# Pairs of expert blocks, a summed norm, and seven raw weight buffers in an encoder layer with a product-key expert FFN

## The chip, the cores and the metric

The kernel runs on one core of one Trainium2 chip. The metric is the device time of one execution in microseconds, and the median over repeated executions is compared. Besides those, one execution was taken with the hardware profiler; all durations below come from it.

## The reference

One layer works on 512 tokens of 1,024 channels: a norm, one input projection, two token mixers (latent attention and a bidirectional state-space scan) merged by gates, an output projection, and then an expert FFN. The part in which most of the time lies is the FFN, which takes for each token and each of 8 heads the 16 best of 16,384 experts:

```python
def peer(h, w_query, sub_keys, w_down, w_up):
    q = (hf @ w_query).reshape(T, PEER_HEADS, 2, PEER_HALF)
    scores = jnp.einsum('thnd,hnkd->thnk', q, sub_keys)
    s_top, i_top = lax.top_k(scores, PEER_TOPK)
    cand = s_top[:, :, 0, :, None] + s_top[:, :, 1, None, :]
    cand_idx = i_top[:, :, 0, :, None] * N_KEYS + i_top[:, :, 1, None, :]
    best, pos = lax.top_k(cand.reshape(T, PEER_HEADS, -1), PEER_TOPK)
    idx = jnp.take_along_axis(cand_idx.reshape(T, PEER_HEADS, -1), pos, axis=-1)
    gate = jax.nn.softmax(best, axis=-1)
    # per token: act = gelu(x . w_down[idx]) * gate;  y = sum act * w_up[idx]

def reference(x, ...):
    h = rmsnorm(x, norm_mix)
    h_q, h_kv, k_r, u_ssm, gates = jnp.split(h @ w_in, IN_SPLITS, axis=-1)
    y_attn = mla(h_q, h_kv, k_r, ...) @ w_o_attn
    z = jax.nn.gelu(s5_bidir(u_ssm, ...)) @ w_glu
    y_ssm = (z[..., :SSM_WIDTH] * jax.nn.sigmoid(z[..., SSM_WIDTH:])) @ w_o_ssm
    g = jax.nn.sigmoid(gates)
    x = x + (g[:, :, 0, :] * y_attn + g[:, :, 1, :] * y_ssm) @ w_out
    x = x + peer(rmsnorm(x, norm_ffn), w_query, sub_keys, w_down, w_up)
    return rmsnorm(x, final_norm)
```

## The kernel before

**Arithmetic.** Every large product is made of fp16 halves: ScalarE writes the high half of a weight tile from its fp32 copy (`whi`), VectorE the low half (`wlo`), and TensorE multiplies three times (high by high, low by high, high by low). A weight tile of 128x1024 thus costs one load of 512 KB into a raw buffer, one ScalarE and one VectorE instruction, and the raw buffer is free again when VectorE has made the low half.

**The front** (`front`) computes the norm, the projections, both mixers and the merge. It begins with the sum of squares of x: 8 squares on ScalarE, each followed by 4 matmuls against a column of ones, then 4 square roots, a reciprocal, diagonal matrices and a matmul that spreads the result over the partitions; then the first two weight tiles, u0 and u1, meet the normed activations. `Stream` holds the list of all weight tiles of the front in the order of use and three raw buffers: `lo()` makes the low half of tile i and then issues loads up to tile i+3. Late in the front stand the attention's output projections (`oa0` to `oa7`, 256 KB each) and the GLU ones (`z0` to `z7`, with `os0` to `os7`), among which tiles of `w_out` (`wo`) and `w_query` (`wq`) that are kept for later are loaded and split.

**The experts** (`experts`, `Peer`) work in two ways. For the first 128 tokens the chosen rows of `w_down` and `w_up` are gathered with indirect DMAs on GpSimd (256 fetches of 128 rows, 512 KB each, into ten buffers) and used on VectorE, one instruction of 128x1024 for each fetch. The other 384 tokens are multiplied with all experts, in 128 blocks of 128. `ph1(i)` is the down product of block i (24 matmuls of 384 columns) and its gelu, which ScalarE writes into a slot: 13 slots of 128x384 in `area`, then 35 ring slots. `ph2(i)` is the up product (18 matmuls of 512 columns into six open PSUM banks); before it, `prep` loads the block's `w_up` and its gates (`Gb`, 192 KB, rows of 256 B from `gd` in HBM), VectorE multiplies slot and gates, ScalarE writes the high half `ph`, VectorE the low half `pl`. The gates in `gd` are made before by `onehot`: 24 tiles of 16 tokens, each four VectorE instructions of 128x2048 (`ej`, `eg` and twice `eg` by the gates) and four quarters of 8 small matmuls with a ScalarE copy each.

**What sets the order.** On TensorE, VectorE and ScalarE the order is written out: a list of units (ph1 and ph2) is run by `step()`, which prepares a unit up to three units ahead of its matmuls. While `onehot` is at work, the units are ph1 with the quarters shared out among them; 18 ph1 lie before that stage and `gtail` = 5 behind it, and all slots (35 + 13 = 48) are full when the stage of ph2 begins. So m = 48 - 18 - 5 = 25 ph1 lie within it. From there on ph2(i) follows ph2(i-1), with a ph1(nx) before it while nx < i + 35. A planner with a cost for each unit on TensorE (`tp`) and VectorE (`td`) puts the last top-k and then the gather's rows between the units, as long as `td < tp + lead`; `gcap` caps the rows per unit. DMA issues on SP and GpSimd are ordered by the framework, and SP's queue is in order: an issue that waits for a buffer holds up all behind it.

## Time and profile before

| | us |
|---|---|
| median of 3 runs | 1563.29 |
| lowest, highest | 1563.12, 1567.69 |
| the profiled execution | 1559.74 |
| its span, first to last instruction | 1558.0 |
| TensorE busy in the span | 1502.0 |
| VectorE busy in the span | 1296.7 |

The span is the time between the first and the last instruction; the execution's own time is 1.74 us longer, and the median of the timed runs lies 3.55 us above that. A busy TensorE is not always one at its peak, since matmuls are pipelined and their ends are modelled. In a table by stage the row gives, for each engine, busy time and instructions, then the granted clock of TensorE (1.00 is 2.4 GHz, 0.50 is 1.2 GHz), the mean busy share of the DMA engines and what they moved.

### The profile page before, as it was taken

The numbers are of one execution on the slowest core, as the hardware profiler recorded it, in microseconds if no ns is written. First come the engines' busy times: TensorE is split into PE (matmuls) and PEld (weight loads), VectorE is DVE, ScalarE is ACT, GpSimd is POOL, SyncE is SP. The second block draws the span as 40 slices with busy tenths as digits, with TensorE's granted clock in tenths as the row PEclk, the third lists the DMA queues.
The fourth block names the chain that finished last, engine by engine and source line by source line (L and its number), as shares of the span: only waits on it lengthen the run. The fifth ranks groups of instructions, "written<-read, shape, count | busy, mean of one in ns | idle before, by whom it ended". The sixth has DMA issues, their size and how long they took to land. (4 is left out here: it accounts for less than half of the span.)

```text
span 1558.0 us, 26141 instructions
## 1 busy us (share of the span) xinstructions
PE 1502.0 (96%) x9921; PEld 854.9 (55%) x9921; DVE 1296.7 (83%) x2571; ACT 742.9 (48%) x1117; POOL 374.5 (24%) x300
## 2 busy tenths in 40 slices
PE   8999999889989999999999999999999999999997
PEld 5547665448676567664444555555555555554433
DVE  4889688555999999986987988888888888888886
ACT  5456765554345479883432443333333333333334
POOL 0100100000000000000026654444555445444310
PEclk9999999999999999999999999999999999999999
DMA  5532622764103347769669999999999999999984
GB/s 192 129 97 49 94 69 90 238 201 157 42 15 125 125 140 284 277 252 332 177 218 389 385 385 366 349 347 348 367 344 354 348 345 368 351 311 323 324 270 147
DMA packets 201135, 378.64 MB, mean 243 GB/s; under 512 B 112305, under 2 KB 117809, under 8 KB 199985
## 3 DMA queue, kind: packets, MB, share of 16 engines
q1 hardware_dynamic: 159904, 231.50, 44.5%
q0 software_dynamic: 39520, 142.59, 26.9%
q10 hardware_dynamic: 1584, 2.88, 0.6%
q8 instruction: 77, 1.26, 0.3%
q14 instruction: 50, 0.40, 0.1%
HBM read 340.25 MB, written 36.14 MB: 242 GB/s over the span
## 5 line engine op out<-in xcount | busy, mean ns | idle before, releaser
L456 DVE SCALAR_TENSOR_TENSOR wlo<-raw,whi 128x1024 f16<-128x1024 f32 x256 | 311.9, 1220 | 125.3 <-ACT whi L453 124.2
L453 ACT ACTIVATE whi<-raw 128x1024 f16<-128x1024 f32 x256 | 262.0, 1050 | 168.7 <-DMA raw<-w_up 94.6
L1514 PE MATMUL ya<-whi,ph 128*128 128x512 f16 x768 | 291.9, 380 | 8.1 <-ACT ph L1502 6.1
L1515 PE MATMUL ya<-wlo,ph 128*128 128x512 f16 x768 | 291.8, 380 | 2.9 <-DVE wlo L456 2.6
L1516 PE MATMUL ya<-whi,pl 128*128 128x512 f16 x768 | 291.8, 380 | 1.0
L1545 POOL DMA_INDIRECT row<-w_dn,gidx x78 | 104.7, 1342 | 625.4 <-ACT whi L453 537.2
L543 PEld LDWEIGHTS <-wlo 128*128 128x128 f16 x1272 | 124.6, 98 | 111.7 <-DVE wlo L493 9.9
L541 PEld LDWEIGHTS <-whi 128*128 128x128 f16 x1272 | 124.6, 98 | 105.1 <-ACT whi L485 11.3
L542 PEld LDWEIGHTS <-whi 128*128 128x128 f16 x1272 | 124.6, 98 | 91.3 <-issue 1.3
L1502 ACT ACTIVATE ph<-Gb 128x384 f16<-128x384 f32 x128 | 66.5, 520 | 214.9 <-DVE Gb L1501 195.7
L1545 POOL DMA_INDIRECT row<-w_up,gidx x78 | 107.5, 1378 | 122.0 <-DVE area L1560 96.5
L1516 PEld LDWEIGHTS <-pl 128*128 128x128 f16 x768 | 75.3, 98 | 101.3 <-DVE pl L1503 11.7
L541 PE MATMUL rps<-hhl,whi 128*128 128x384 f16 x384 | 125.6, 327 | 2.6 <-ACT whi L453 2.6
L543 PE MATMUL rps<-hhl,wlo 128*128 128x384 f16 x384 | 125.9, 328 | 2.0 <-DVE wlo L456 2.0
L1514 PEld LDWEIGHTS <-ph 128*128 128x128 f16 x768 | 75.3, 98 | 94.4 <-ACT ph L1502 10.2
L542 PE MATMUL rps<-hhl,whi 128*128 128x384 f16 x384 | 125.6, 327 | 0.0
L1515 PEld LDWEIGHTS <-ph 128*128 128x128 f16 x768 | 75.3, 98 | 87.7 <-issue 2.6
L1444 ACT COPY stg<-rps 128x512 f32<-128x512 f32 x96 | 98.3, 1077 | 16.4 <-PE rps L1442 15.7
L543 PE MATMUL rota<-hhl,wlo 128*128 128x384 f16 x320 | 104.3, 326 | 1.4 <-DVE wlo L456 1.4
L541 PE MATMUL rota<-hhl,whi 128*128 128x384 f16 x320 | 104.3, 326 | 0.0
L542 PE MATMUL rota<-hhl,whi 128*128 128x384 f16 x320 | 104.3, 326 | 0.0
L541 PE MATMUL rotb<-hhl,whi 128*128 128x384 f16 x320 | 104.3, 326 | 0.0
(370 smaller groups left out, 2994.4 us busy)
## 6 DMA issues: line engine op xcount, KB each, us to landing
raw<-w_dnT SPq DMA_DIRECT2D x128, 512.0 KB
raw<-w_up SPq DMA_DIRECT2D x128, 512.0 KB
gd<-stg SPq DMA_DIRECT2D x6, 4096.0 KB
Gb<-gd SPq DMA_DIRECT2D x128, 192.0 KB
raw<-w_g SPq DMA_DIRECT2D x16, 512.0 KB
raw<-w_out SPq DMA_DIRECT2D x8, 512.0 KB
raw<-w_query SPq DMA_DIRECT2D x8, 512.0 KB
x<-x SPq DMA_DIRECT2D x8, 512.0 KB
```

The costliest lines, as they stand in the source:

```text
L453: E.nc.scalar.activation(hi, raw, AF.Copy, scale=scale)
L456: E.nc.vector.scalar_tensor_tensor(lo, raw, scale, hi, op0=OP.mult, op1=OP.subtract)
L541: E.nc.tensor.matmul(o, lhsT=lh, rhs=rh, start=start and i == 0, stop=False)
L542: E.nc.tensor.matmul(o, lhsT=lh, rhs=rl, start=False, stop=False)
L543: E.nc.tensor.matmul(o, lhsT=ll, rhs=rh, start=False, stop=stop and i == n - 1)
L1444: nc.scalar.copy(self.stg[:, :, t0:t0 + TQ].rearrange("p i t -> p t i"), o)
L1502: hi, lo = halves(E, wp, raw, D, "up", 3, SU, lambda: nc.scalar.activation(ph, P, AF.Copy, scale=scale))
L1514: nc.tensor.matmul(o, lhsT=ph[:, ts], rhs=hi[:, ns], start=f, stop=False)
L1515: nc.tensor.matmul(o, lhsT=ph[:, ts], rhs=lo[:, ns], start=False, stop=False)
L1516: nc.tensor.matmul(o, lhsT=pl[:, ts], rhs=hi[:, ns], start=False, stop=l)
L1545: E.nc.gpsimd.indirect_dma_start(out=r, out_offset=None, in_=E.a[src], in_offset=bass.IndirectOffsetOnAxis(ap=E.gidx[:, k:k + 1], axis=0))
```

## The change

Four things change.

1. **Pairs.** Slots, gates, `ph` and `pl` are made for two blocks: one load of 384 KB (rows of 512 B), one product, one high and one low half of 128x768 at every even block; the product is written into the slot instead of the gates' buffer. The ring has 17 pairs (34 slots) and the area 6 (12 slots), so the slots are 46 instead of 48.
2. **Planner.** Costs of ph1, ph2 and a gathered row are new numbers, and `gcap` goes from 1.42 to 1.45.
3. **The sum of squares** is added up on VectorE (7 additions of 128x512) before 4 matmuls; one square root takes all four columns; u0's high half moves ahead of it, and the low halves of u0 and u1 come behind the diagonals.
4. **Seven raw buffers** in the memory that the state-space part has left, for the tiles of the front from there to `os7`.

```diff
         self.raw, self.parts, self.open = [], [], []
+        self.wide, self.end = None, 0
+    def widen(self, pool, last):
+        self.wide, self.end = pool, self.at[last] + 1
...
             n = self.items[i][2]
-            r = self.pool.tile([128, 1024], F32, name="raw", tag="wraw", bufs=self.bufs)
+            pool, bufs = (self.wide, 7) if i < self.end else (self.pool, self.bufs)
+            r = pool.tile([128, 1024], F32, name="raw", tag="wraw", bufs=bufs)
             self.E.dma(r[:, :n], self.items[i][1])
...
             self.E.R.until(self.E.R.td, n / 900.0)
-            while len(self.raw) < min(i + 1 + self.bufs, len(self.items)):
+            while len(self.raw) < min(i + 1 + (7 if len(self.raw) < self.end else self.bufs), len(self.items)):
                 self.load()
...
             nc.scalar.activation(warm, E.eps, AF.Sqrt)
-            sso = [ps.tile([128, 1], F32, name="pss", tag="ps") for _ in range(4)]
             for k in range(KT):
                 nc.scalar.activation(sq[:, k], xT[:, k], AF.Square)
-                for c in range(4):
-                    nc.tensor.matmul(sso[c], lhsT=sq[:, k, c * 128:c * 128 + 128], rhs=E.ones[:, 0:1],
-                                     start=(k == 0), stop=(k == KT - 1))
+                if k:
+                    V.tensor_add(sq[:, 0], sq[:, 0], sq[:, k])
+            sso = ps.tile([128, 4], F32, name="pss", tag="ps")
+            for c in range(4):
+                nc.tensor.matmul(sso[:, c:c + 1], lhsT=sq[:, 0, c * 128:c * 128 + 128], rhs=E.ones[:, 0:1],
+                                 start=True, stop=True)
+            st.hi()
             ssx = wk.tile([128, 4], F32, name="ssx", tag="ssc", bufs=2)
-            for c in range(4):
-                nc.scalar.activation(ssx[:, c:c + 1], sso[c], AF.Sqrt, scale=1.0 / D, bias=E.eps)
-            st.hi()
-            st.hi()
+            nc.scalar.activation(ssx, sso, AF.Sqrt, scale=1.0 / D, bias=E.eps)
             V.reciprocal(ssx, ssx)
             r = spread(E, ps, diagonals(E, wk, ssx))
+            w01 = [st.get(f"u{i}") for i in range(2)]
             uT = sp.tile([128, 4, T], F32, name="uT", tag="u8")
...
-            st.lo()
             hn = h_of(0)
-            w01 = [st.get(f"u{i}") for i in range(2)]
             for k in range(KT):
...
             R.weights2()
+            w2c = ExitStack()
+            st.widen(w2c.enter_context(E.pool(name="w2", bufs=1)), "os7")
             R.os = [fp.tile([128, 8, 512], F16, name="os", tag=x) for x in ("hhi", "hlo")]
...
             st.upto("os7")
+            w2c.close()
             upc.close()
...
         self.bank = bank
-        self.ring = [rp.tile([128, self.TD], F32, name=f"ring{i}") for i in range(self.NR)]
+        self.ring = [rp.tile([128, 2, self.TD], F32, name=f"ring{i}") for i in range(self.NR // 2)]
         self.iom = rp.tile([128, self.NB, 2], F16, name="iom")
...
         self.area = gp.tile([128, 5 * D], F32, name="area")
-        self.first = [self.area[:, i * self.TD:i * self.TD + self.TD] for i in range(5 * D // self.TD)]
+        n = 2 * self.TD
+        self.first = [self.area[:, i * n:i * n + n].rearrange("p (b t) -> p b t", b=2) for i in range(5 * D // n)]
+    def pair(self, j):
+        n = len(self.first)
+        return self.first[j] if j < n else self.ring[(j - n) % len(self.ring)]
     def slot(self, i):
-        n = len(self.first)
-        return self.first[i] if i < n else self.ring[(i - n) % self.NR]
+        return self.pair(i // 2)[:, i % 2]
...
     def gload(self, i):
-        while len(self.G) <= min(i, self.NB - 1):
-            g = self.gr.tile([128, self.TD // self.TC, self.TC], F32, name="Gb", bufs=5)
-            self.E.dma(g, self.E.gd.rearrange("c j i t -> j i c t")[:, len(self.G)])
-            self.G.append(g.rearrange("p c t -> p (c t)"))
+        while 2 * len(self.G) <= min(i, self.NB - 1):
+            k = 2 * len(self.G) * self.TC
+            g = self.gr.tile([128, self.TD // self.TC, 2, self.TC], F32, name="Gb", bufs=3)
+            self.E.dma(g.rearrange("p c b t -> p c (b t)"),
+                       self.E.gd.rearrange("c j i t -> j c (i t)")[:, :, k:k + 2 * self.TC])
+            self.G.append(g)
...
             up, scale = E.a["w_up"][i * 128:i * 128 + 128], SP / SG
-            ph = wp.tile([128, self.TD], F16, name="ph", bufs=3)
-            pl = wp.tile([128, self.TD], F16, name="pl", bufs=3)
             raw = rload(E, wp, up, D, "up")
             self.gload(i + 2)
-            P = self.G[i]
-            V.tensor_tensor(P, self.slot(i), P, op=OP.mult)
-            hi, lo = halves(E, wp, raw, D, "up", 3, SU, lambda: nc.scalar.activation(ph, P, AF.Copy, scale=scale))
-            V.scalar_tensor_tensor(pl, P, scale, ph, op0=OP.mult, op1=OP.subtract)
+            if i % 2:
+                hi, lo = halves(E, wp, raw, D, "up", 3, SU)
+            else:
+                G, R = self.G[i // 2], self.pair(i // 2)
+                byc = lambda x: x.rearrange("p b (c t) -> p c b t", t=self.TC)
+                self.ph = wp.tile([128, 2, self.TD], F16, name="ph", bufs=3)
+                self.pl = wp.tile([128, 2, self.TD], F16, name="pl", bufs=3)
+                V.tensor_tensor(byc(R), byc(R), G, op=OP.mult)
+                hi, lo = halves(E, wp, raw, D, "up", 3, SU,
+                                lambda: nc.scalar.activation(self.ph, R, AF.Copy, scale=scale))
+                V.scalar_tensor_tensor(self.pl, R, scale, self.ph, op0=OP.mult, op1=OP.subtract)
+            ph, pl = self.ph[:, i % 2], self.pl[:, i % 2]
             w.extend((hi, lo, ph, pl))
...
         quarters = [quarter(s, q) for s in range(len(tiles)) for q in range(NQ)]
-        n1 = P.NR + len(P.first)
+        n1 = P.NR + 2 * len(P.first)
         m = n1 - nx - E.gtail
...
         while nx < n1:
-            add(P.ph1(nx), 3.95, 1.14)
+            add(P.ph1(nx), 3.95, 1.25)
             nx += 1
...
             if nx < P.NB and nx < i + P.NR:
-                add(P.ph1(nx), 3.95, 1.14)
+                add(P.ph1(nx), 3.95, 1.25)
                 nx += 1
-            add(P.ph2(i), 3.9, 2.2)
+            add(P.ph2(i), 3.9, 1.25 if i % 2 else 3.15)
         last = P.units[-3:]
...
                         R.bg.pop(0)
-                        assert k > mid + len(P.first)
+                        assert k > mid + 2 * len(P.first)
                         tk.close()
...
                     P.pace(1.0)
-                    td += 1.2
+                    td += 1.29
                     room -= 1.0
...
     E.wr = 3
-    E.nring = 35
+    E.nring = 34
     E.gtail = 5
...
     E.f1 = 2.25
-    E.lead, E.gcap = 1.0, 1.42
+    E.lead, E.gcap = 1.0, 1.45
     E.gskip = (1, 2, 6, 8, 9, 10, 12, 13, 14, 15)
```

On ScalarE the front begins, of before and then of now, as follows (`sqx` are the squares, `ssx` the roots, `whi` and `u1hi` the high halves of u0 and u1).

```order
L694 ACTIVATE sqx<-xTs 128x512 x8
L700 ACTIVATE ssx<-pss,eps 128x1 x4
L485 ACTIVATE whi<-raw 128x1024
L485 ACTIVATE u1hi<-raw 128x1024
L440 ACTIVATE hhi<-htmp 128x512 x6
```

```order
L699 ACTIVATE sqx<-xTs 128x512 x8
L491 ACTIVATE whi<-raw 128x1024
L708 ACTIVATE ssx<-pss,eps 128x4
L491 ACTIVATE u1hi<-raw 128x1024
L440 ACTIVATE hhi<-htmp 128x512 x6
```

The high half of u0 now comes before the root, and one root instruction replaces four.

On SP's queue, from the last load of the old buffers at `oa1` on, first of before and then of now (a raw tile's number tells its buffer's maker: in the second list 3095, 3496 and 3534 are in the three old buffers, the others in the seven new ones).

```order
L1860 DMA raw_3044<-w_oa 128x512
L1860 DMA nrow_3133<-nffn_row 128x1024
L1860 DMA subk_3132<-subk 128x1024
L1860 DMA raw_3122<-w_out 128x1024
L1860 DMA raw_3160<-w_oa 128x512
L1860 DMA raw_3163<-w_query 128x1024
L1860 DMA raw_3187<-w_oa 128x512
L1860 DMA raw_3190<-w_out 128x1024
L1860 DMA raw_3214<-w_oa 128x512
L1860 DMA raw_3217<-w_out 128x1024
L1860 DMA raw_3241<-w_oa 128x512
```

```order
L1881 DMA raw_3138<-w_query 128x1024
L1881 DMA raw_3140<-w_oa 128x512
L1881 DMA raw_3142<-w_out 128x1024
L1881 DMA raw_3095<-w_out 128x1024
L1881 DMA raw_3144<-w_oa 128x512
L1881 DMA raw_3147<-w_out 128x1024
L1881 DMA raw_3171<-w_oa 128x512
L1881 DMA nrow_3106<-nffn_row 128x1024
L1881 DMA subk_3105<-subk 128x1024
L1881 DMA raw_3496<-w_query 128x1024
L1881 DMA raw_3534<-w_query 128x1024
L1881 DMA raw_3174<-w_query 128x1024
```

Seven loads now stand ahead of the first that needs a new buffer to come free, and three tiles of `w_query` for after `os7` (3496, 3534 and, next after the last row shown, 3537) are loaded into the old buffers as these come free.

On VectorE, at the end of the `onehot` stage and the first blocks of ph2, before and now:

```order
L456 SCALAR_TENSOR_TENSOR wlo<-raw,whi 128x1024
L1427 TENSOR_TENSOR ej<-iom,gij 128x2048
L1429 TENSOR_TENSOR eg<-iom,gij 128x2048
L1431 TENSOR_TENSOR eg<-eg,ghl 128x2048 x2
L456 SCALAR_TENSOR_TENSOR wlo<-raw,whi 128x1024 x5
L1501 TENSOR_TENSOR Gb<-area,Gb 128x384
L456 SCALAR_TENSOR_TENSOR wlo<-raw,whi 128x1024
L1503 SCALAR_TENSOR_TENSOR pl<-Gb,ph 128x384
L1501 TENSOR_TENSOR Gb<-area,Gb 128x384
L456 SCALAR_TENSOR_TENSOR wlo<-raw,whi 128x1024
L1503 SCALAR_TENSOR_TENSOR pl<-Gb,ph 128x384
```

```order
L1444 TENSOR_TENSOR eg<-eg,ghl 128x2048 x2
L1440 TENSOR_TENSOR ej<-iom,gij 128x2048
L1442 TENSOR_TENSOR eg<-iom,gij 128x2048
L1444 TENSOR_TENSOR eg<-eg,ghl 128x2048 x2
L456 SCALAR_TENSOR_TENSOR wlo<-raw,whi 128x1024 x5
L1520 TENSOR_TENSOR area<-area,Gb 128x6x2x64
L456 SCALAR_TENSOR_TENSOR wlo<-raw,whi 128x1024
L1523 SCALAR_TENSOR_TENSOR pl<-area,ph 128x768
L456 SCALAR_TENSOR_TENSOR wlo<-raw,whi 128x1024
L1520 TENSOR_TENSOR area<-area,Gb 128x6x2x64
```

Between the last two tiles of the stage no ph1's `wlo` stands any more (there are 21 in the stage instead of 23, and m = 46 - 18 - 5 = 23 ph1 instead of 25), and the product and `pl` stand at every second block at twice the size.

## Rows read from the trace of the kernel before

**Rows 1.** By stage: length, each engine's busy us, granted clock, DMA share, GB/s.
```profile
14.50:18.40 3.90, 3.75 (x18) 3.67 (x18) 0.00 (x0) 0.90 (x4) 0.00 (x0) 1.00 0.00 0
294.00:341.00 47.00, 40.41 (x169) 15.30 (x167) 29.06 (x39) 24.77 (x39) 0.00 (x0) 0.96 0.68 211
302.50:305.90 3.40, 3.40 (x9) 1.22 (x8) 2.25 (x3) 1.72 (x3) 0.00 (x0) 0.50 0.89 283
549.80:691.00 141.20, 141.02 (x1330) 98.61 (x1328) 139.50 (x120) 122.07 (x140) 0.00 (x0) 1.00 0.62 239
806.00:853.00 47.00, 41.51 (x216) 20.67 (x215) 35.01 (x53) 12.96 (x20) 33.27 (x25) 0.99 1.02 378
853.00:1412.00 559.00, 559.00 (x3006) 294.31 (x3005) 481.33 (x608) 211.52 (x297) 284.43 (x206) 1.00 1.01 354
1412.00:1460.00 48.00, 47.87 (x222) 21.62 (x221) 40.74 (x55) 16.57 (x22) 19.31 (x15) 1.00 1.00 326
1460.00:1528.00 68.00, 62.17 (x271) 25.17 (x270) 59.48 (x76) 27.07 (x38) 12.96 (x10) 1.00 0.87 275
```

**Rows 2.** The first 24 us in order of time: start, us, instruction, idle before.
```profile
4.44 13.81 PE L696 MATMUL pss<-ones,sqx 128*128 128x1 f32 x64 [4.44 <-ACT sqx L694]
...
8.40 3.30 ACT L694 ACTIVATE sqx<-xTs 128x512 f32<-128x512 f32 x5 [1.48 <-DMA xTs<-xT]
...
17.01 0.26 ACT L700 ACTIVATE ssx<-pss,eps 128x1 f32<-128x1 f32 x1 [5.31 <-PE pss L696]
...
18.87 0.69 DVE L563 TENSOR_TENSOR dgs<-ident,ssx 128x512 f32<-128x512 f32 x1
...
19.53 1.23 DVE L493 SCALAR_TENSOR_TENSOR wlo<-raw,whi 128x1024 f16<-128x1024 f32 x1
...
19.62 2.08 PE L572 MATMUL pbc<-dgs,ones 128*128 128x128 f32 x8 [1.37 <-DVE dgs L563]
...
21.81 1.40 DVE L710 SCALAR_TENSOR_TENSOR htmp<-xTs,nmix,pbc 128x512 f32<-128x512 f32 x2
...
23.26 0.59 PE L725 MATMUL pu<-hhi,whi 128*128 128x512 f16 x1 [1.57 <-ACT hhi L440]
```

**Rows 3.** Waits from 294 to 341 us: who for whom, us, times, longest.
```profile
PEld L543 <- DVE wlo L493: 6.2, 10, 0.8
ACT whi L485 <- DMA raw<-w_glu: 5.7, 4, 2.4
PE pp L541 <- ACT whi L485: 5.2, 5, 2.0
ACT whi L485 <- DMA raw<-w_oa: 4.9, 5, 2.0
```

**Rows 4.** The `onehot` stage, 549.8 to 691 us, by line: busy, mean ns, idle.
```profile
L1442 PEld LDWEIGHTS <-ej 128*128 128x128 f16 x737 | 48.6, 97 | 16.2 <-DVE eg L1431 6.2
...
L456 DVE SCALAR_TENSOR_TENSOR wlo<-raw,whi 128x1024 f16<-128x1024 f32 x24 | 29.2, 1218 | 2.4 <-ACT whi L453 2.4
```

**Rows 5.** From 853 to 1412 us by line, VectorE: busy us, mean ns, idle.
```profile
L456 DVE SCALAR_TENSOR_TENSOR wlo<-raw,whi 128x1024 f16<-128x1024 f32 x145 | 177.0, 1221 | 75.3 <-ACT whi L453 74.8 <-issue 0.3
...
L1560 DVE SCALAR_TENSOR_TENSOR area<-row,gco,area 128x1024 f32<-128x1024 f32 x61 | 78.0, 1278 | 0.0
...
L1501 DVE TENSOR_TENSOR Gb<-ring,Gb 128x384 f32<-128x384 f32 x74 | 40.8, 552 | 0.0
```

**Rows 6.** The page, part 3: DMA queue, packets, MB, share of 16 engines' span.
```profile
q1 hardware_dynamic: 159904, 231.50, 44.5%
q0 software_dynamic: 39520, 142.59, 26.9%
```

**Rows 7.** The chain that ended last, two places: start us, us, what.
```profile
828.60 19.57 DMA raw<-w_up
...
1447.83 1.07 ACT whi L453
1450.18 7.49 DMA raw<-w_up
```

## The prediction

> **What bounds the kernel now.** I read the table by stage first, then the waits of the stages that lose time, then the chain of waits. In the table one compares a stage's length with TensorE's busy time. From 853 to 1412 us the two are equal, 559.00 of 559.00 [rows 1]: there only fewer matmuls could help, and the change removes none. TensorE is short of work in four places. Before the first real matmul at 23.26 us it waits for the norm [rows 2]. From 294 to 341 us it is busy 40.41 of 47.00, and 3.40 us of that run at half clock [rows 1]; the waits show high halves that wait for loads [rows 3]. From 806 to 853, where the gather starts, it is idle 5.49 us, and from 1412 to 1528, where ph2 runs alone, 0.13 + 5.83 = 5.96 us [rows 1]; there the chain of waits goes through loads of w_up [rows 7]. One stage reads differently from its busy share: from 549.8 to 691 TensorE is busy 141.02 of 141.20, but VectorE is too (139.50), and the small weight loads idle 6.2 us on VectorE's `eg` [rows 1, 4]. VectorE paces that stage, and TensorE's busy time there is padding of pipelined matmuls.
>
> **The change, part by part.**
>
> Front. The squares end at 8.40 + 3.30 = 11.70 us, and then 64 recorded matmul passes, 13.81 / 64 = 0.216 us each, run until 18.25 [rows 2]. Now VectorE adds up the squares. No row shows such an addition; the nearest, 128x512 fp32 on VectorE, took 0.69, and a square 0.66, so it keeps pace and ends at about 12.4. Eight passes are left: 1.7, to 14.1. Root 0.26 and reciprocal with hand-overs 0.4: 14.8; diagonals 0.69: 15.5; spread 2.08: 17.6. Beside it VectorE makes the two low halves, 2 x 1.23, to 18.0, then one `htmp` of 0.70, to 18.7, and ScalarE's half of that (0.6) lets TensorE start at 19.3 instead of 23.3. The one thing that could stand in the way is u0's load, whose high half is now ahead of the root. From 14.50 to 18.40 the DMA engines move nothing [rows 1], so the three tiles issued so far had landed by 14.5; u0 is the first. If it came only at 14.5, the root would slip by 1.1. So 2.9 to 4.1; I take 4.0, since u0 is first of three. What follows is paced from there, its loads too, so the shift is kept.
>
> Seven raw buffers. Of the 6.59 us idle in 294 to 341, 5.2 are waits for a high half, the rest for low halves behind them, and the high halves waited 5.7 and 4.9 us for w_glu and w_oa [rows 1, 3]. Three buffers leave one load a round trip per three tiles; the stage moved 211 GB/s where another reaches 378 [rows 1]. With seven, the tiles for the next four products are under way. I take 5.5 us of the waits, and 1.7 for the 3.40 us at half clock that came after the longest wait [rows 1]: 7.2 in all. What is late next is ScalarE or VectorE, with 24.77 and 29.06 us of work in 47 [rows 1], less than TensorE's 38.7 at full clock. SP's queue now holds three loads of w_query ahead of oa6, and they wait for old buffers; oa2 to oa5 are ahead of them, four products of 12 matmuls, some 10 us of cover. Bounds: 2 (only every third wait goes) to 8.3 (all).
>
> Two slots fewer. Two ph1 leave the stage that VectorE paces, where each costs it one low half, 1.22 us [rows 4]: 2.4 gained. They come back in the stage that TensorE fills. There 145 low halves stand for 145 units in 559 us [rows 1, 5], so a unit takes 3.86, and ph1 and ph2 have the same number of columns (24 x 384 = 18 x 512): 7.7 lost. Net +5.3, with bounds 0 (first rival) and 6.
>
> Gates by two blocks. The gather's queue took 26.9% of 16 x 1558 us for 142.59 MB, 47 us per MB [rows 6]. Of q1's 231.50 MB, the gates are 25.2 in 98,304 packets of 256 B; at 47 us per MB the other 206.3 MB took 9,700 of q1's 11,090 us, which leaves 14 ns for a packet of 256 B, 0.68 us of all engines per block. A packet of 512 B then costs between 14 and 28 ns (no row has it), so a block gains 0.34 to nothing; I take the half, 0.17. It counts where loads are late. At the gather's start one load of w_up took 19.57 us [rows 7] and some six blocks pass: 1.0 of the 5.49 idle, with bounds of 5.5 gained and 1 lost (a load of 384 KB ahead of a raw one). The Trainium skill, "DMA: Bandwidth & Descriptors", Specifications, wants 512 B or more per transfer for line rate, by which 256 B would cost as much as 512. By that rule the place gains 2.0 and the sum would be 1.0 us lower; no row here has 512 B alone.
>
> Pairs on VectorE and ScalarE. Product and `pl` take 552 ns at 384 and a low half 1,221 at 1,024 [rows 5]; between them 768 comes to 0.95, so two blocks cost 2 x 0.95 + 2 x 1.22 = 4.34 instead of 4.65. I cost this at nothing: VectorE is busy 481 of 559 us in the main stage [rows 1], and a unit is prepared three units ahead. If the product's runs of 64 halved its rate, two blocks would cost 5.3, and with 2.64 gathered rows at 1.28 [rows 5] VectorE would need 8.7 per 7.7 us where ph2 runs alone: that stage's gain below would go. Behind the `onehot` stage the first two loads of gates carry 768 KB where three carried 576: 0, between -1.5 and +1.5.
>
> Gather's pace and the last stage. Per unit the planner allowed (3.9 - 2.2) / 1.2 = 1.42 rows where ph2 runs alone, now (3.9 - 2.2) / 1.29 = 1.32. With 0.524 MB per row and raw tile and 0.197 of gates, a block asked 1.46 MB there, 4.5 us at the 326 GB/s of 1412 to 1460; now 1.41, 4.0 at the main stage's 354 [rows 1]. The shortfall against 3.86 falls from 0.6 to 0.15 per block. And the gather is over sooner: 256 rows at 1.45 per unit are 177 units instead of 180, in a list two units longer, five units or 19 us more before the end. Three units of lead (11.6 us) then outlast the shortfall. I take 5.0 of the 5.96 idle, bounds 0 and 6.
>
> Sum: -4.0 - 7.2 + 5.3 - 1.0 - 5.0 = -11.9 us. The profiled execution took 1559.74, of which the span is 1558.0: it becomes 1547.8. The median of the runs lies 3.55 above the profiled one, so I predict 1551.4.
>
> **The rivals.**
>
> A. The `onehot` stage is TensorE's after all (141.02 of 141.20 busy [rows 1]). Then two ph1 less there save what they cost later, 0 instead of +5.3: 1546.1. Against it stand VectorE's 139.50 and the weight loads that wait for it.
>
> B. The new buffers bring 2 instead of 7.2: oa6 and what follows stand behind the w_query loads that wait for old buffers, or ScalarE's order delays the halves anyway. 1556.6. For it speaks that low halves, too, were waited for, 6.2 us by the weight loads [rows 3].
>
> C. The DMA engines have no more to give in the main stage: their share is 1.01 at 354 GB/s [rows 1]. Now a ph1 with a ph2 asks 2 x 0.524 + 0.197 + 2.9 x 0.524 = 2.76 MB in 7.71 us, 359 GB/s. If 354 were the ceiling, each such pair would take 7.81, over 75 pairs 7.5 us, and the last stage would start without lead, 5.0 not gained: 1563.9. Against it: 378 GB/s from 806 to 853 [rows 1]. The Trainium skill, "DMA: Bandwidth & Descriptors", Specifications, gives HBM a limit of about 358 GB/s per core, by which 359 would not fit; the row of 378 is above it, and the measurement decides.
>
> D. Slower: in the last stage every odd block's w_up stands in SP's queue behind 384 KB of gates, 192 KB more than now. With a load, a high and a low half, two buffers make a loop that serves two blocks; the wait of 5.96 us over 17 such loops, after a lead of 11.6, says that a loop ran 1.03 over 7.71, so its load took 6.45 on average (7.49 in [rows 7]). If gather and raw loads share the engines, 192 KB cost 1.2 us more: 2.23 over per loop, over 14 loops less the lead 19.6 idle, instead of 1.0. That is 18.6 on top: 1570.0. It decides from an odd load above 6.2 us (5.4 for the pace, 0.8 that the lead bears). Against it: each even load has that much less ahead of it, and the shortfall of bytes is smaller.
>
> **How the numbers follow.** The forecast gets 0.53, A 0.10, B 0.15, C 0.08, D 0.07, and 0.07 stay for what is not on the list, on either side. About 0.3%, 4.7 us, is what a measurement of this kernel can tell from no change, so faster means under 1558.6: the forecast, A, most of B and a part of the rest, 0.77. Within are C, the rest of B and a part of the rest, 0.13; slower are D and a part of C and the rest, 0.10. The forecast's own terms span 1546 to 1556. The range must hold 8 in 10: from 1544 (A with the gather's start gained in full) to 1561 (B with its own bounds), with C and D left out.
>
> **What would show it.** Front: the first matmul of 512 columns near 19.3 us. Buffers: the stage of oa and z some 7 us shorter, no wait of a high half for w_oa or w_glu, no half clock in it. Slots: 21 low halves between first and last `ej`, the stage about 138.8 us, TensorE's weight loads idle on `eg` for more than 6.2 us, and the full stage 7.7 us longer. Gates: q1 with some 49,000 packets fewer, and its share lower. End: TensorE's idle time where ph2 runs alone under 1.5 us, the last gathered row well before it. The forecast is wrong if TensorE shows idle time in the main stage (C), if loads of w_up take over 6.2 us at odd blocks (D), or if the oa stage keeps its waits (B).

## The result, and the profile after

The changed kernel took 1546.78 us (median of 4 runs, 1544.91 to 1549.62), the kernel before beside it 1564.32 us; the ratio is 0.9886, with a 95% interval of 0.9861 to 0.9911. Forecast were 1551.4 us, 1544 to 1561. The profiled execution took 1545.21 us with a span of 1543.4, 14.5 us less than before; 11.9 were forecast.

The table by stage of the changed kernel, with the columns of [rows 1]: the `onehot` stage, the gather's start, the main stage, and two stretches of ph2 alone.

```profile
541.00:680.30 139.30, 133.55 (x1281) 93.72 (x1279) 136.99 (x117) 117.70 (x135) 0.00 (x0) 1.00 0.62 235
794.00:862.00 68.00, 63.09 (x331) 32.29 (x329) 52.95 (x69) 20.24 (x28) 47.69 (x32) 0.97 1.02 384
862.00:1402.00 540.00, 540.00 (x2916) 285.07 (x2915) 468.28 (x525) 197.82 (x251) 300.65 (x206) 1.00 0.98 359
1404.00:1450.00 46.00, 46.00 (x215) 20.83 (x213) 35.17 (x40) 15.78 (x18) 19.41 (x13) 1.00 0.92 315
1450.00:1518.00 68.00, 67.56 (x313) 30.09 (x311) 56.89 (x57) 27.12 (x32) 7.27 (x5) 1.00 0.76 258
```

One reads three things here. The main stage (third line) is still full, now at 359 GB/s. The gather's start still loses 4.91 us, where [rows 1] had 5.49. And the last line holds 313 matmuls in 68 us, in which [rows 1] had 271: in this trace the idle time where ph2 runs alone is gone.

The first 20 us, in order of time, answer to [rows 2].

```profile
8.09 3.88 DVE L701 TENSOR_TENSOR sqx<-sqx 128x512 f32<-128x512 f32 x5 [0.79 <-ACT sqx L699]
...
11.39 1.06 ACT L491 ACTIVATE whi<-raw 128x1024 f16<-128x1024 f32 x1 [0.64 <-DMA raw<-w_u]
12.02 1.87 PE L704 MATMUL pss<-ones,sqx 128*128 128x1 f32 x8 [12.02 <-DVE sqx L701]
13.93 0.26 ACT L708 ACTIVATE ssx<-pss,eps 128x4 f32<-128x4 f32 x1 [1.48 <-PE pss L704]
...
15.25 2.07 PE L578 MATMUL pbc<-dgs,ones 128*128 128x128 f32 x8 [1.36 <-DVE dgs L569]
...
17.39 1.40 DVE L717 SCALAR_TENSOR_TENSOR htmp<-xTs,nmix,pbc 128x512 f32<-128x512 f32 x2
...
18.84 0.58 PE L730 MATMUL pu<-hhi,whi 128*128 128x512 f16 x1 [1.52 <-ACT hhi L440]
```

VectorE's additions keep pace with the squares and end at 11.97; u0 had landed by 11.39, so its high half delayed nothing; the first matmul of 512 columns comes at 18.84 instead of 23.26.

The late front: in the kernel before and the changed one, the two stretches from the first `oa` product to the first product with `zg`, and from there to the first with `wq`; for the changed one also the ten microseconds from 293.6 on.

```profile
288.40:345.90 57.50, 46.25 (x194) 17.59 (x193) 33.82 (x46) 30.72 (x49) 0.00 (x0) 0.97 0.67 208
345.90:380.20 34.30, 34.30 (x441) 28.63 (x441) 18.97 (x29) 16.26 (x25) 0.00 (x0) 0.95 0.54 176
```

```profile
284.06:335.20 51.14, 44.87 (x194) 19.02 (x193) 31.60 (x42) 28.68 (x44) 0.00 (x0) 0.93 0.71 244
335.20:370.80 35.60, 33.31 (x441) 27.04 (x440) 20.39 (x32) 17.31 (x29) 0.00 (x0) 1.00 0.49 149
...
293.60:303.60 10.00, 7.58 (x22) 2.65 (x23) 6.84 (x9) 7.66 (x11) 0.00 (x0) 0.66 0.95 329
```

Together 91.8 us before and 86.74 now: 5.1 us gained, not 7.2; 6.27 us of the first stretch are still without a matmul. What took the rest stands in the changed kernel's order of time (`sigb` are the gates' rows of 256 KB that the `oa` products are multiplied by, read back from HBM):

```profile
284.88 0.33 ACTq L797 DMA_DIRECT2D gates<-sig  x1
...
285.31 1.15 ACTq L1030 DMA_DIRECT2D sigb<-gates  x2
...
293.56 0.63 ACT L1038 ACTIVATE sigb<-sigb 128x512 f32<-128x512 f32 x1 [4.18 <-DMA sigb<-gates]
...
295.04 0.61 ACT L491 ACTIVATE whi<-raw 128x512 f16<-128x512 f32 x1
...
295.71 0.61 PE L547 MATMUL pp<-oT,whi 128*128 128x512 f16 x1 [3.90 <-ACT whi L491]
```

The same two steps in the kernel before:

```profile
289.56 1.08 ACTq L1023 DMA_DIRECT2D sigb<-gates  x2
...
293.58 0.63 ACT L1031 ACTIVATE sigb<-sigb 128x512 f32<-128x512 f32 x1
```

From issue to use `sigb` took 4.02 us before and 8.25 now. (Before, ScalarE didn't wait for it: it loaded a table of 1.28 us until 293.56. A trace with the same old front, the one below with the planner's numbers alone, has this load landed 2.94 us after its issue.) The prefetch of the seven buffers stands ahead of it; ScalarE, whose queue is in order, waits 4.18 us, the next high half comes late, TensorE idles 3.90 us, and the clock falls behind that (0.66 mean over 10 us). A wait for weights has become a wait for a small transfer that the weights delay.

The last stage, from the last ph1's last matmul to the last product, in the kernel before and the changed one:

```profile
1404.93:1550.89 145.96, 139.90 (x632) 60.23 (x630) 120.84 (x163) 56.13 (x84) 34.88 (x27) 1.00 0.85 272
```

```profile
1403.54:1536.36 132.82, 132.38 (x613) 59.49 (x612) 105.49 (x115) 51.08 (x66) 26.68 (x18) 1.00 0.75 255
```

It holds 35 blocks before and 34 now, since the ring is a block shorter. An experiment below ran 35 blocks there in 136.00 us with TensorE busy throughout, so 34 take 132.1: lost were 10.0 us before and 0.7 now. This is the shortest of the eight traces, this one and seven of the runs below, that have the changed kernel's code in this stage: they took 132.8 to 136.4 us, so 0.7 to 4.3 were lost, 2.3 in the mean, and the gain there is 5.7 to 9.3 us. GpSimd's count shows 27 gathered rows issued there before, 18 now.

By stretches, the 14.5 us of the profiled execution come out like this (the `onehot` stage is taken from its first to its last small matmul):

| stretch | before | after | change | of it |
|---|---|---|---|---|
| to the first 128x512 matmul | 23.26 | 18.84 | -4.4 | front |
| to the first `oa` product | 265.1 | 265.2 | +0.1 | |
| to the first `wq` product | 91.8 | 86.8 | -5.0 | seven buffers |
| to the first small matmul | 176.0 | 176.3 | +0.3 | |
| `onehot` stage | 139.0 | 137.2 | -1.8 | two ph1 fewer |
| to the second block of ph2 | 32.1 | 31.0 | -1.1 | |
| to the 31st block | 187.3 | 190.0 | +2.7 | one ph1 more (3.86), gather's start |
| to the last ph1 | 490.3 | 498.1 | +7.8 | one ph1 and one block of ph2 more |
| to the last product | 146.0 | 132.8 | -13.1 | one block of ph2 fewer (3.88), idle gone |

### The profile page after: what moved, and what is told of

It reads as the page before. It is cut to its first block, busy times and chain, and to the rows that moved or that the text cites. A ratio compares the mean times of both kernels' runs of the same rounds, so it can differ in the third digit from the quotient of the medians.

```text
span 1543.4 us, 25496 instructions
## 1 busy us (share of the span) xinstructions
PE 1482.4 (96%) x9865; PEld 842.9 (55%) x9865; DVE 1292.7 (84%) x2450; ACT 728.2 (47%) x1050; POOL 399.0 (26%) x300
## 4 chain that ended last, share of the span: by engine, by line
PE 64%; DVE 19%; DMA 9%; ACT 5%; issue 3%; POOL 0%; SPq 0%; ACTq 0%; DVEq 0%; POOLq 0%
PE ya L1537 8%; PE ya L1535 8%; PE ya L1536 8%; DMA raw<-w_up 4%; PE rota L549 3%; PE rotb L547 3%; PE rotb L549 3%; PE rotb L548 3%; PE rota L547 3%; PE rota L548 3%; DVE wlo L456 3%; PE pg L547 2%; PE pg L548 2%; PE pg L549 2%; PE pp L549 1%
## 5 line engine op out<-in xcount | busy, mean ns | idle before, releaser
L548 PEld LDWEIGHTS <-whi 128*128 128x128 f16 x1272 | 124.4, 98 | 92.4 <-issue 1.3
L1566 POOL DMA_INDIRECT row<-w_up,gidx x78 | 121.1, 1552 | 97.1 <-DVE area L1581 79.8
L547 PE MATMUL rps<-hhl,whi 128*128 128x384 f16 x368 | 119.9, 326 | 2.4 <-ACT whi L453 2.4
L549 PE MATMUL rps<-hhl,wlo 128*128 128x384 f16 x368 | 120.2, 327 | 2.0 <-DVE wlo L456 2.0
L548 PE MATMUL rps<-hhl,whi 128*128 128x384 f16 x368 | 120.0, 326 | 0.0
L1522 ACT ACTIVATE ph<-ring 128x768 f16<-128x768 f32 x58 | 48.7, 840 | 132.7 <-DVE ring L1520 132.7
L547 PE MATMUL rota<-hhl,whi 128*128 128x384 f16 x328 | 107.1, 327 | 0.0
L548 PE MATMUL rotb<-hhl,whi 128*128 128x384 f16 x328 | 107.1, 326 | 0.0
L547 PE MATMUL rotb<-hhl,whi 128*128 128x384 f16 x328 | 107.1, 326 | 0.0
L548 PE MATMUL rota<-hhl,whi 128*128 128x384 f16 x328 | 107.1, 326 | 0.0
```

Of the source, the lines that this page charges most:

```text
L547: E.nc.tensor.matmul(o, lhsT=lh, rhs=rh, start=start and i == 0, stop=False)
L548: E.nc.tensor.matmul(o, lhsT=lh, rhs=rl, start=False, stop=False)
L549: E.nc.tensor.matmul(o, lhsT=ll, rhs=rh, start=False, stop=stop and i == n - 1)
L1522: lambda: nc.scalar.activation(self.ph, R, AF.Copy, scale=scale))
L1566: E.nc.gpsimd.indirect_dma_start(out=r, out_offset=None, in_=E.a[src], in_offset=bass.IndirectOffsetOnAxis(ap=E.gidx[:, k:k + 1], axis=0))
```

## The experiments

Each kernel was timed beside the kernel before, whose medians were 1563.85, 1563.67 and 1563.6 us in the three groups.

**The changed kernel again, and the changed kernel without the seven buffers.** As it is, beside the last group:

> The changed kernel once more, beside the others on the same chip. Both theories: within 0.3% of its first median, 1542 to 1551 us, and from the last ph1 to the last product 132 to 137 us, since runs with the same last stage have given 132.8 to 136.4.

It took 1548.16 us (6 runs, 1545.67 to 1553.61; ratio 0.9899, 0.9878 to 0.992). Its late front took 88.3 us in the profile, with the same wait (3.52 us idle at 296.9), and the last stage 133.9. Its span was 1548.3 us, 9.7 less than before where the first trace has 14.5. One trace thus carries several us of chance: six traces with the changed kernel's front took 86.5 to 89.3 us from the first `oa` to the first `wq` product, four with the old front 90.8 to 95.4. The other leaves the wide pool out:

```diff
-            w2c = ExitStack()
-            st.widen(w2c.enter_context(E.pool(name="w2", bufs=1)), "os7")
```

> The changed kernel without the seven raw buffers (three all through the front). Theory 1 (the buffers gave the 4.9 us that the trace of the changed kernel shows between the first oa product and the end of the front): that part is longer by 4.9 us, about 1552 us, with waits of high halves for w_oa and w_glu back and sigb landing some 4 us after its issue. Rival (part of the 4.9 us comes from the earlier start of the front or from chance in the clock): 1 to 3 us longer.

1554.73 us (ratio 0.9941, 0.9922 to 0.996), with the late front in two stretches of

```profile
285.70:340.00 54.30, 45.87 (x193) 17.71 (x192) 32.36 (x42) 29.47 (x44) 0.00 (x0) 0.97 0.66 210
340.00:378.10 38.10, 35.00 (x441) 28.71 (x440) 21.63 (x34) 18.37 (x30) 0.00 (x0) 0.96 0.52 175
```

92.4 us against 86.7 and 88.3: the buffers bring 4.1 to 5.7 us there, and 6.6 to 8.0 in the medians. Theory 1 holds; the earlier front, which this kernel has too, is not the source.

**Is it `sigb`?** First the two early loads alone, issued behind the gate before the last:

```diff
             for i, m in enumerate(E.grest[len(E.grest) - n:]):
                 gate(m)
                 if i == 0:
                     s5_turn(E, ps, ysp)
+                    sigs = [sig(0), sig(1)]
...
-            sigs = [sig(0), sig(1)]
             for m in range(8):
```

> The changed kernel with the first two loads of sigb issued behind the gate before the last instead of behind the last one, some 7 us earlier; nothing else moves. Theory 1 (in the changed kernel the 3.90 us of idle at 295.71 us and the half clock behind it come from sigb, which was issued at 285.31 behind some 2.3 MB of weight loads and landed only at 293.53): the first sigmoid follows right behind the first product, the idle goes, the half clock with it or in part, and the time from the first oa product to the end of the front falls by 4 to 7 us against the changed kernel, the whole to about 1540 us. Rival (the high half of the next oa tile is late anyway, for ScalarE's order or its own load): the wait is then one of whi for w_oa or wo, and the whole falls by 0 to 2 us.

1549.12 us (1543.92 to 1551.18), no difference that the medians can tell; the late front took 47.94 + 35.50 = 83.4 us. The first sigmoid waits no longer, but behind it stands

```profile
293.59 0.33 ACTq L1019 DMA_DIRECT2D sigb<-gates  x1
293.96 1.06 ACT L491 ACTIVATE wo<-raw 128x1024 f16<-128x1024 f32 x1 [2.78 <-DMA gates<-sig]
```

The third `sigb` takes the buffer of the last gate, whose store is just as late behind the weights, and ScalarE waits for that. So `sigb` had buffers of its own next, from the memory of the seventh raw one (lines that are not shown set six raw buffers and open their pool a gate earlier):

```diff
+                    w2 = w2c.enter_context(E.pool(name="w2", bufs=1))
+                    st.widen(w2, "os7")
+                    sigs = [sig(j) for j in range(3)]
...
-                s = wk.tile([128, T], F32, name="sigb", tag="t2", bufs=3)
+                s = w2.tile([128, T], F32, name="sigb", tag="sigb", bufs=3)
...
-                if m < 6:
-                    sigs.append(sig(m + 2))
+                if m < 5:
+                    sigs.append(sig(m + 3))
```

> The changed kernel with three buffers of their own for sigb, the first three of its loads issued behind the gate before the last, and six raw buffers instead of seven (the memory of the seventh holds sigb). With the two early loads alone the first sigmoid no longer waited, but ScalarE then waited 2.78 us for the store of the last gate, whose buffer the third sigb took: idle 2.62 us at 295.6 and 3.4 us of half clock stayed, and the stretch from the first oa product to the first w_query product took 83.4 us (86.8 in the changed kernel, 91.8 before). Theory 1 (it is transfers of 256 KB that land behind megabytes of prefetched weights, and nothing else, that holds the oa products): no wait for sigb or the store is left, and the stretch takes 79 to 81 us. Rival (behind that, ScalarE's or VectorE's own order paces the products): 82 to 84 us.

1547.93 us; 50.03 + 35.81 = 85.8 us there, which neither theory had. No product waits long any more, but each waits a little, and the reason is the edit: the load three products ahead needs the buffer that VectorE's product frees only then, and ScalarE's queue stands still for it.

```profile
294.31 0.33 ACTq L1019 DMA_DIRECT2D sigb<-gates  x1
294.68 1.06 ACT L491 ACTIVATE wq<-raw 128x1024 f16<-128x1024 f32 x1 [1.83 <-DVE mixed L1041]
```

With two ahead after the first three:

```diff
-                if m < 5:
-                    sigs.append(sig(m + 3))
+                if 0 < m < 6:
+                    sigs.append(sig(m + 2))
```

> The changed kernel with three buffers of their own for sigb and six raw buffers, the first three sigb loads issued a gate earlier, as in the run before it of that kind, but every further load of sigb is issued two products ahead, into a buffer that has come free by then. With three ahead ScalarE waited 1.83 us at two products (and 1.13 once) for the product of VectorE that frees the buffer, and the products followed each other at 3.9 us instead of 2.6. Theory 1 (that wait of my own making held them): the stretch from the first oa product to the first w_query product takes 79 to 82 us, where the changed kernel took 86.8, and the whole is 4 to 7 us shorter than the changed kernel beside it. Rival (ScalarE's order paces the products in any case): 83 to 87 us, and no difference on the whole.

```profile
285.35:330.80 45.45, 42.41 (x195) 18.39 (x193) 31.70 (x42) 28.73 (x44) 0.00 (x0) 1.00 0.75 274
330.80:366.30 35.50, 33.38 (x442) 27.12 (x441) 20.39 (x32) 17.51 (x30) 0.00 (x0) 1.00 0.47 150
```

80.95 us at full clock, as theory 1 said, 5.8 and 7.4 less than in the two traces of the changed kernel, and 4.9 less than with three ahead, from which it differs only in when `sigb` is issued. So it is shown that the late transfers of 256 KB, the load and the store, cost the buffers' gain its second half. On the whole it took 1545.92 us (6 runs, 1541.93 to 1551.36; ratio 0.9887, 0.9864 to 0.9909) against 1548.16 beside it: the lowest median of all, but 2.2 us is less than these runs can tell apart, and the 4 to 7 us that I expected of the whole were not confirmed.

**What did two ph1 fewer cost?**

```diff
-    E.gtail = 5
+    E.gtail = 3
```

> The changed kernel with three instead of five ph1 behind the onehot stage, so that 25 ph1 lie in it as before. Theory 1 (VectorE paces that stage): it grows from 137.5 us by 2.4 to about 140, and the two ph1 are gone from the part that TensorE fills, 7.7 us less there, unless the gates that ph2 waits for come too late; the whole falls by 0 to 5 us, about 1543 us. Rival (TensorE paces the stage): it grows by 7.7 to about 145, and the whole stays within 1 us or, if ph2's first gates are late, becomes up to 5 us longer.

Seen through the 24 `ej` of VectorE (first and last start), in the kernel before, the changed one and this one:

```profile
L1427 DVE TENSOR_TENSOR ej<-iom,gij x24: 1215/1218/1218, 549.8 to 686.1; 128x2048 f16<-128x2048 f16 x24
```

```profile
L1440 DVE TENSOR_TENSOR ej<-iom,gij x24: 1217/1219/1221, 540.7 to 674.8; 128x2048 f16<-128x2048 f16 x24
```

```profile
L1440 DVE TENSOR_TENSOR ej<-iom,gij x24: 1216/1218/1219, 544.0 to 680.2; 128x2048 f16<-128x2048 f16 x24
```

136.3, 134.1 and 136.2 us: two ph1 are worth 2.1 us in that stage, near VectorE's 2 x 1.22 and far from TensorE's 2 x 3.86. The other traces say the same within 0.03 us: 136.25 to 136.28 with 25 ph1, 134.12 to 134.14 with 23. That settles who paces it. But the kernel took 1551.24 us (1550.41 to 1557.16), for

```profile
710.85 0.61 PE L1535 MATMUL ya<-whi,ph 128*128 128x512 f16 x1 [6.07 <-ACT ph L1522]
...
719.30 0.59 PE L1535 MATMUL ya<-whi,ph 128*128 128x512 f16 x1 [4.24 <-ACT ring L1494]
```

The five ph1 behind the stage cover the way of the last gates to HBM and back; with three, TensorE waits there for what it saved. The store was then split so that the first blocks' gates go first:

```diff
-                E.dma(E.gd[s * TS // TC], self.stg)
+                c, n = s * TS // TC, 16
+                E.dma(E.gd[c][:, :n], self.stg[:, :n])
+                E.dma(E.gd[c][:, n:], self.stg[:, n:])
```

> The changed kernel with three ph1 behind the onehot stage instead of five, and every store of the gates split so that the rows of the first 16 blocks go first (512 KB, then 3.5 MB). With three ph1 alone the stage grew by 1.7 us only, but the first gates came late: the last store of 4 MB took 12 us to land, and TensorE was idle 6.07 and 4.24 us. Theory 1 (two ph1 in the stage cost 1.7 us instead of 7.7, and only the landing of the store hid that gain): the first gates come some 8 us earlier, the two waits shrink to under 3 us in sum, and the whole is 2 to 6 us shorter than the changed kernel, 1541 to 1545 us. Rival (the loads of w_dn and w_up that stand behind the same 4 MB hold the blocks anyway): the waits stay at 6 us or more, and the whole comes to 1548 to 1552 us.

1551.95 us; the two waits are 5.04 and 2.45 us, as the rival had it. SP's queue shows why: after the two stores it issues no load of gates before the larger one is done.

```profile
688.84 0.81 SPq L1883 DMA_DIRECT2D gd<-stg  x2
691.36 1.60 SPq L1883 DMA_DIRECT2D raw<-w_dnT  x2
701.06 0.33 SPq L1883 DMA_DIRECT2D raw<-w_up  x1
701.44 2.15 SPq L1883 DMA_DIRECT2D Gb<-gd  x2
```

Whether the gates waited for the second store itself or only stood behind the `w_up` load ahead of them is not settled.

**The last stage: planner, pairs or rows?** The planner's old numbers in the changed kernel, and the new ones alone in the kernel before (in the first, `gcap` and the costs of ph1, ph2 and row all go back; in the second ph2 stays at 2.2):

```diff
-                    td += 1.29
+                    td += 1.2
```

> The changed kernel with the planner's old numbers (ph1 1.14, ph2 2.2, row 1.2, cap 1.42); pairs, front and seven raw buffers stay. Theory 1 (the 9.5 us lost where ph2 runs alone went because the new numbers spread the rows thinner and end the gather sooner): most of that idle is back, 5 to 9 us longer, about 1553 us, all of it behind 1400 us. Rival (the pairs did it: fewer packets and shorter VectorE work): the last stage stays without idle time, within 2 us of the changed kernel, about 1547 us.

```diff
-                    td += 1.2
+                    td += 1.29
```

> The kernel before with the planner's new numbers alone (ph1 1.25, row 1.29, cap 1.45; ph2 stays at 2.2). From the last ph1 to the last product took 146.0 us before, 132.8 with the whole change and 139.6 with the pairs under the old numbers. Theory 1 (the two halves add up, each because fewer bytes are asked per block where ph2 runs alone): about 139 us, and the whole some 7 us shorter than before, about 1557 us. Rival (the new numbers help only with the pairs' smaller VectorE load): 144 to 148 us there and no gain on the whole, about 1564 us.

The first took 1551.59 us (ratio 0.9919, 0.9887 to 0.995, which overlaps with that of the changed kernel), the second 1565.2 (1.0005, 0.999 to 1.002: no change). Their last stages:

```profile
1409.35:1549.00 139.65, 135.56 (x614) 59.68 (x612) 110.69 (x122) 51.52 (x66) 32.63 (x22) 0.99 0.75 257
```

```profile
1410.40:1556.20 145.80, 140.51 (x632) 61.09 (x630) 115.25 (x157) 56.33 (x84) 28.56 (x23) 0.99 0.81 254
```

Lost are 7.5 us of 34 blocks and 9.8 of 35. So the numbers alone bring nothing on the whole and 0.2 us here, although four rows fewer are left for the stage; the pairs under the old numbers gain 2.5; both together 5.7 to 9.3, by the eight traces. That is more than the sum, but by no more than these runs can settle: the two stages above are one trace each, and each holds 3.4 us at half clock behind a wait (0.99 in the rows), some 1.5 us that the eight don't lose. That pairs and numbers need each other is likely, and not shown.

Then the rows themselves, in the kernel before. Left out are the last 22 rows of `w_up` (in the first kernel fetch and use, in the second the use):

```diff
+            if src == "w_up" and k >= 106:
+                self.rows.append((f, k, None))
+                continue
```

> The kernel before; the last 22 rows of w_up of the gather (of 256 rows) are left out, fetch and VectorE instruction both, so the outputs of 128 tokens lack a part. In the kernel before 27 rows were issued behind the last ph1, and from there to the last product TensorE lost some 10 us against back-to-back products (146.0 us for 35 blocks of 3.88). Theory 1 (the rows cause that loss): 137 to 139 us there. Rival (the loop of two w_up buffers, load, high half, low half, is too long by itself): 143 us or more.

```profile
1409.90:1545.90 136.00, 136.00 (x632) 61.54 (x630) 94.45 (x141) 55.10 (x84) 6.68 (x5) 1.00 0.68 206
```

No idle time at all: the 10.0 us were due to the rows that were left over for that stage, and not to the loop of the two `w_up` buffers. (1553.66 us on the whole.)

```diff
-                f(k, r)
+                if f != self.gup or k < 106:
+                    f(k, r)
```

> The kernel before; the same 22 rows are fetched, but VectorE's instruction on each is left out, so the outputs of 128 tokens lack a part. Theory 1a (the bytes of the rows delay the w_up loads): as before, 143 to 146 us from the last ph1 to the last product. Theory 1b (VectorE's 1.28 us per row, which stand in its queue ahead of low halves and so of buffers coming free): 137 to 140 us. Between them: both.

159.6 us there and 1578.37 on the whole: worse than with VectorE's work. The edit broke something else. Rows without a user are fetched in bursts, and SP's queue, in which a load of x into `area` waits for one of them to land, stands still with the `w_up` loads behind it:

```profile
1434.93 0.39 SPq L1861 DMA_DIRECT2D Gb<-gd  x1
1459.41 0.33 SPq L1861 DMA_DIRECT2D area<-x  x1
1459.85 0.37 SPq L1861 DMA_DIRECT2D raw<-w_up  x1
```

```profile
SPq L1861 <- DMA area<-w_up,gidx: 31.4, 3, 24.1
```

TensorE's wait at its end is 16.62 us. Of the other 7 us of the 23.6 lost, some 4 are half clock (21 matmuls in 8.6 us), and some 3 remain. Since the fetches also came at other times, this run can't tell whether bytes or VectorE's time did it: that stays open.

**Packets of 512 B.** Pairs as they are, but the gates fetched by two loads with rows of 256 B:

```diff
-            self.E.dma(g.rearrange("p c b t -> p c (b t)"),
-                       self.E.gd.rearrange("c j i t -> j c (i t)")[:, :, k:k + 2 * self.TC])
+            for b in range(2):
+                self.E.dma(g[:, :, b], self.E.gd.rearrange("c j i t -> j i c t")[:, 2 * len(self.G) + b])
```

> The changed kernel with the gates of a pair loaded by two transfers with rows of 256 B instead of one with rows of 512 B; the pair's product and halves stay as they are. Theory 1 (the pairs help in the last stage through the DMA engines, by fewer packets): from the last ph1 to the last product it takes 136 to 140 us instead of 132.8, and the gates' queue has its larger share again; 1550 to 1554 us. Rival (they help through VectorE's and ScalarE's shorter work, or by loads that come two blocks ahead): within 1 us of 132.8, about 1547 us.

1552.51 us (ratio 0.9919, 0.9897 to 0.994), at the range that theory 1 gave, but not for its reason: the last stage took 135.6 us, inside the 132.8 to 136.4 of the kernels that share it. 2.6 to 4.0 us more than in the changed kernel's two traces went between the second and the 31st block of ph2, where the gather starts; here are the first of those traces and this run:

```profile
715.42:905.41 189.99, 185.08 (x955) 93.50 (x954) 169.72 (x359) 70.10 (x91) 76.80 (x52) 0.99 0.85 307
```

```profile
716.98:910.97 193.99, 187.78 (x955) 94.34 (x954) 172.07 (x360) 70.74 (x91) 77.23 (x53) 0.97 0.90 307
```

The clock column tells most of it: 0.97 for 0.99 is some 3.4 us, at half clock behind a wait of 2.95 us for a high half at 852.8. One such wait in one trace is too little to call it the price of the smaller packets. The queue's rows, of the changed kernel and of this one:

```profile
q1 hardware_dynamic: 109728, 231.49, 43.1%
```

```profile
q1 hardware_dynamic: 159904, 231.50, 45.0%
```

At spans of 1543.4 and 1552.1 us that is 10,643 and 11,175 us of engine time for the same bytes: 532 us for 50,176 packets more, 10.6 ns each. By [rows 6] (44.5%, 11,093 us) it is 9.0.

## Why the prediction was right, and where not

**Front, -4.0.** Measured -4.4 at the first large matmul and -4.3 at the first `oa` product. Each step came within 0.4 us. Ten traces with the new front have that matmul at 18.5 to 19.6, four with the old one at 23.2 to 23.3: -4.1 in the mean. That the shift is kept is less sure. The first `oa` product came at 284.1 to 287.8 us in the seven of them that are alike up to there, and at 287.0 to 289.6 in the four, 2.7 us apart in the mean.

**Seven buffers, -7.2.** Measured -5.0, and -5.7 between the means of the traces with either front. The waits for `w_oa` and `w_glu` went, as said. The step that failed is "what is late next is ScalarE or VectorE": late next was `sigb`, a transfer of 256 KB that the forecast did not look at, since in the kernel before it cost nothing. It gave the 3.90 us at 295.7 and the half clock back. Rival B's 2 us were too few. Of its two causes, the loads of `w_query` ahead of `oa6` held no `oa` product up; ScalarE's order did delay a half, through a load that B did not name. The sum also started from too little: the 169 matmuls of [rows 1], at 0.216 us each, need 36.5 of those 47.00 us. So 10.5 were lost there, half clock included, where I took 6.59 + 1.7 = 8.3 for all, and the run with `sigb` two ahead gained 10.9.

**Two slots fewer, +5.3.** Measured +7.7 in the stages that TensorE fills (+3.86, +7.77, -3.88) and 1.8 to 2.1 gained in the `onehot` stage, +5.6 to +5.9. Its weight loads wait there for `eg` for 12.7 us instead of 6.2, as the forecast had it. Rival A falls with the run of 25 ph1 in that stage: a ph1 there costs 1.07 us instead of 3.86. That the median of 1546.78 lies next to A's 1546.1 is chance.

**Gates by two blocks, -1.0.** To the 31st block +2.7 with 3.86 for one ph1 more: -1.2. Six traces with this stage unchanged took 188.0 to 191.4 us there, so the gain lies between 3.2 and nothing, and -1.2 confirms no more than that. The packet of 512 B was bounded between 14 and 28 ns; a saving of 9 to 10.6 ns per pair of 256 B puts it at 17 to 19, a little on the cheap side of the middle that I took. The Trainium skill, "DMA: Bandwidth & Descriptors", Specifications, wants 512 B or more for line rate. The run with 256 B rows agrees in the DMA engines' time, 450 to 532 us more; a price in the kernel's time it doesn't show.

**Pairs on VectorE, 0.** Product and `pl` of 128x768 took 952 and 951 ns, the 0.95 of the forecast. VectorE is busy 468 of 540 us in the main stage and TensorE waits for it nowhere there: right.

**Last stage, -5.0.** Measured -9.3 in the first trace, 5.7 to 9.3 in eight. That the gathered rows cause the loss was right, as the run without the last 22 shows. The size was not, and the rows of the trace would have given it: I took 0.13 + 5.83 us of idle time from busy time, but where matmuls stand apart each modelled end counts as busy. The count tells more: from 1412 to 1460 there are 222 matmuls in 47.87 us, 0.216 each, and 271 x 0.216 = 58.5 of the 68 us behind that [rows 1], 9.5 lost instead of 5.83. I had read the padding in the `onehot` stage and forgotten it here. The account of bytes is not confirmed: the planner's numbers were to bring most of the gain, and alone they brought none; 256 B rows lengthened nothing there; and whether a row costs by its bytes or by its 1.28 us on VectorE stays open. So does what in the pairs helps this stage.

**The end.** The terms add up to -11.9 and the trace to -14.5, with the buffers 2.2 short and the last stage 4.3 over; the second trace of the changed kernel comes to -9.7. So the sum came out well in part because its errors offset each other. The other 2 us of the 4.6 between forecast and median are in the assumption that the median lies 3.55 us above the profiled execution; this time it was 1.57.

**Rivals C and D.** The main stage ran 540.00 of 540 us busy at 359 GB/s, the very figure that C held out of reach. The Trainium skill's limit of about 358 GB/s per core (same page and section) did not bind here, with 359 over 540 us and 384 over 68; the page derives it by halving a stack's 716 GB/s between two cores, and this program runs on one. Loads of `w_up` right behind gates of two blocks did land later, as D had it: in the last stage of the first trace 12 of them after 5.2 us in the mean, the 17 others after 4.4. Three of the 12 took more than 6.2 us (6.83 the longest), but TensorE waited for none of them: the stage has one wait, 0.4 us for `pl`.

## What to carry to other kernels

A deeper prefetch lengthens the wait of every small transfer issued behind it: before adding buffers, list what else must land in that stretch, issue it earlier, and look at whose buffer it takes. Read lost time as length less count times the interval of back-to-back matmuls, not as length less busy time. And before work is moved into a stage that another engine paces, ask what the work that leaves its old place was covering.

## What was unexpected

From issue to use, 256 KB took at most 4.02 us before and 8.25 us behind the prefetch, and a store of the same size held up ScalarE by 2.78 us through a buffer alone. TensorE's clock shows in the time of equal runs: of the four runs of the changed kernel the two with a mean granted clock of 0.992 and 0.993 took 1545.21 and 1544.91 us, the two with 0.990 1549.62 and 1548.35. In its six later runs the extremes agree (0.995 took 1545.67, 0.987 took 1553.61), but one with 0.993 took 1550.09, so the clock is not all of it. Some 4 us, about the 0.3% that a comparison can resolve, can come from where the clock falls, and a trace of one execution has to be read with that in mind.
